# All input products as Strassen quads, with the attention steps between them: a gated hybrid decoder layer on one NeuronCore

## The chip, the cores and the metric

The kernel runs on one core of one Trainium2 chip. A core has TensorE (PE in the profile, its weight loads PEld), VectorE (DVE), ScalarE (ACT), GpSimd (POOL) and SyncE (SP, which here only issues DMAs), an on-chip memory SBUF and the accumulators of TensorE, PSUM, in eight banks of 128 x 512 fp32. The metric is the device time of one execution in microseconds (us); lower is better.

## The reference

One layer is computed, for 2048 tokens of width 1024, in fp32:

```
shift, scale, gate = SiLU(c) @ W_ada + b_ada
u = x * (1 + scale) + shift
[q | k | v | attn_gate | pool_in | pool_gate | merge_a | merge_p] = u @ W_in
A = SlidingWindowGQA_with_sinks(q, k, v; relative bias) * SiLU(attn_gate)          -> @ W_attn_proj
P = (GroupLinear(MultiScaleCausalPool(pool_in)) * pool_scale) * SiLU(pool_gate)    -> @ W_pool_proj
y = (sigmoid(merge_a) * A + sigmoid(merge_p) * P) @ W_out * (1 + gate)
out = LayerNorm(alpha * x + y)
```

Attention has 16 query heads of 64 and 2 key/value heads, a window of 128 tokens and a sink per head. The pool windows are 2, 4, 8 and 16 tokens, one for each quarter of the width.

## The kernel before, in words

**Precision.** TensorE works in fp32r, a rounded fp32. So each operand is split into a rounded part hi and a residue lo, and each product of a 128 x 128 weight tile with 128 x 512 columns takes three matmuls, hi*hi, hi*lo and lo*hi (`mm3`, line 137). ScalarE makes hi by a copy, VectorE makes lo by a subtraction (`low`, line 131).

**Strassen quads.** A `Quad` (line 276) takes two output tiles of 128 columns of a weight and 1024 tokens: a 2 x 2 problem in the halves of the inner width (1024 = 2 x 512) and of the tokens. Strassen's form (Winograd's variant) needs 7 products instead of 8; a product (line 339) is 4 slices of 128 times 3 matmuls, 12 matmuls of 512 columns. The moving side stands in seven sets, B11, T1, T2, B21, T3, B22 and T4, each 128 x 4 x (hi, lo) x 512; the weight side is summed by GpSimd (`sum1`, `mid`, `late`, lines 296 to 306) and split just before use (`pair_split`, line 326, and `half_split`, line 332). `front` opens a quad with the products of B11 and T1, `back` does T2, B21, T3, B22 and T4 and hands the four output tiles to a `consume` function. `ring` (line 447) runs groups of two quads; after each product it calls a tick, and a table of hooks by group and tick places all side work (lines 451 to 458). `defer` puts something off by a number of ticks.

**Stages.** The 2048 tokens are two chunks of 1024. For each chunk:
- a gate stage (`first_phase`, `second_phase`): 17 quads, one for k and v and 16 for the four gates; outputs of the gates pass through a sigmoid (line 545) and go to DRAM. In the first chunk the ticks also carry the folding of the pool-mix weights into the pool-input weights (`fold_parts`, kept split in DRAM as `wmix_d`), the rest of the gate modulation and the split sets of the second chunk (`sums_to` with `kept_parts`). In the second they carry the split sets of the output weight and of the first chunk's attention output (`resplit`).
- an attention stage (`attention`, line 724): 64 steps, one per pair of heads and block of 128 queries, with scores, exponentials, normalisation, transposes and the product with v passing through a pipeline of steps. Into each step goes half of a plain projection (`projection`, line 694: 8 slices of 3 matmuls for one tile of 128 columns and 512 tokens): the q tiles and the folded pool-input tiles, 32 per chunk. For this stage k and v stay in SBUF (`kk`, `vv`), and B11, B21, T2 and B22 hold the plain halves of u. Window sums, gating and the Strassen sums of both outputs run on GpSimd (lines 763 to 814).

Then five mix phases run in one ring each: attention and pool projection of chunk 0, the same of chunk 1 (4 quads each, times the merge gates read back from DRAM), and the output product with the LayerNorm (8 quads). From phase to phase the seven sets are exchanged while the last group still runs (`set_steps`, line 488): raw halves come into two spare rooms and are split from there into the sets; where a store already holds split parts (u of chunk 1, attention of chunk 0, the output weight) a half comes as one load of 1 MB (`fill_set`, line 201).

**Order.** Where operations go through `act`, `dve`, `pool`, `pe` and `sp` they stay in program order among themselves (class `Ordered`, line 50); those through `nc.scalar`, `nc.vector` and so on may be moved by the scheduler. Line 56 is therefore the line of most rows of the profile, and tile names tell them apart: `w_set` is a split weight, `set_T`/`set_B` a moving set, `mm`, `lg`, `pt` and `pv` are PSUM tiles (four, two, one and one banks), `L` holds the logits, `ptl` the residue of the transposed probabilities.

## Time and profile before

| what | value |
|---|---|
| time, three runs | 1781.38 us median (1779.84 to 1782.57) |
| profiled execution, first to last instruction (span) | 1776.8 us; the page gives no time of its own around it |
| TensorE busy, 8248 matmuls | 1711.0 us, 96% |
| VectorE, ScalarE, GpSimd busy | 67%, 52%, 45% |
| DMA | 381.31 MB, 215 GB/s on average |
| granted TensorE clock, mean | 0.989 |

A page of the profile lists the busy time of each engine, the span in 40 slices, the DMA queues, the chain of work that ended last, and groups of equal instructions: line, engine, operation, output<-input by tile names, shapes and count, then busy time and mean duration in ns, then the idle time of the engine just before them and what ended it. Other views list the same for a stretch of time, what an engine waited for, and the instructions in order of time. Matmuls overlap in the pipeline, so a matmul's mean duration is longer than the distance from one to the next.

### The profile page before, as it was taken

What the parts mean: (1) busy time and instruction counts of PE and PEld (TensorE: products, weight loads), DVE (VectorE), ACT (ScalarE), POOL (GpSimd) and SP (SyncE); (2) the same over time, 40 slices, a digit from 0 to 9 for tenths busy, and PEclk for the clock granted to TensorE, in tenths of its full rate; (3) what the DMA queues carried; (4) which work ended last, traced back from release to release, by engine and by line L of the source; (5) the groups of instructions that cost most, each with busy time, mean ns of one, the idle gap of its engine ahead of it and who ended that gap; (6) DMA issues with size and microseconds to landing.
All of it is one profiled execution on the core that took longest, in us unless ns stands there. A gap on an engine that the chain in (4) does not pass through costs nothing. (4 is left out here: it accounts for less than half of the span.)

```text
span 1776.8 us, 24983 instructions
## 1 busy us (share of the span) xinstructions
PE 1711.0 (96%) x8248; PEld 1431.2 (81%) x8248; DVE 1199.1 (67%) x2180; ACT 931.5 (52%) x1969; POOL 795.5 (45%) x610
## 2 busy tenths in 40 slices
PE   6899999999999999999999999999989989999996
PEld 5687888888888887788788888888877868788785
DVE  5866665655777787767655367777857686865777
ACT  3543444445777776454444377777734333423451
POOL 3144454441356567534434025456743552364542
PEclk9899999999999999999999999999999999999998
DMA  9265768743354557787776724554886575689432
GB/s 365 98 238 201 256 218 276 255 174 131 113 166 144 171 202 283 269 289 252 257 276 246 247 79 144 165 166 131 296 307 226 184 253 183 219 312 384 168 143 96
DMA packets 181155, 381.31 MB, mean 215 GB/s; under 512 B 18833, under 2 KB 39329, under 8 KB 181025
## 3 DMA queue, kind: packets, MB, share of 16 engines
q1 hardware_dynamic: 174880, 365.76, 59.1%
q0 software_dynamic: 2912, 9.46, 1.4%
q10 hardware_dynamic: 3232, 4.49, 0.9%
q8 instruction: 65, 1.06, 0.2%
q14 instruction: 66, 0.53, 0.1%
HBM read 244.35 MB, written 138.44 MB: 215 GB/s over the span
## 5 line engine op out<-in xcount | busy, mean ns | idle before, releaser
L56 PE MATMUL mm<-set_B,w_set 128*128 128x512 f32 x3240 | 802.3, 396 | 11.8 <-DVE w_set L132 9.0
L56 PEld LDWEIGHTS mm<-set_B,w_set 128*128 128x128 f32 x3240 | 604.5, 189 | 141.8 <-DVE w_set L132 16.0
L56 PE MATMUL lg<-set_T,w_set 128*128 128x512 f32 x2088 | 511.3, 395 | 22.8 <-DVE w_set L132 12.7
L56 PEld LDWEIGHTS lg<-set_T,w_set 128*128 128x128 f32 x2088 | 392.6, 190 | 115.6 <-DVE w_set L132 18.2
L132 DVE TENSOR_TENSOR w_set<-W,w_set 128x1024 fp32r<-128x1024 f32 x162 | 224.7, 1387 | 177.7 <-ACT w_set L328 169.2
L328 ACT CAST w_set<-W 128x1024 fp32r<-128x1024 f32 x162 | 169.8, 1050 | 242.1 <-PE mm L56 182.5
L56 PE MATMUL mm<-set_T,w_set 128*128 128x512 f32 x1080 | 268.7, 397 | 1.3 <-DVE set_T L56 1.3
L56 PEld LDWEIGHTS mm<-set_T,w_set 128*128 128x128 f32 x1080 | 201.9, 190 | 44.2 <-DVE set_T L56 3.0
L297 POOL TENSOR_TENSOR W<-W,A 128x512 f32<-128x512 f32 x56 | 84.8, 1514 | 247.0 <-DMA A<-in_win_dram 66.6
L306 POOL TENSOR_TENSOR W<-W 128x512 f32<-128x512 f32 x56 | 82.0, 1465 | 160.8 <-DVE w_set L132 146.5
L56 DVE TENSOR_TENSOR o<-pv,o 64x128 f32<-64x128 f32 x256 | 72.4, 283 | 92.1 <-ACT o L56 89.3
L56 ACT ACTIVATE L<-L,nm 128x257 f32<-128x257 f32 (+1 forms) x256 | 127.1, 498 | 9.0 <-DVE nm L56 3.6
L301 POOL TENSOR_TENSOR W<-W 128x512 f32<-128x512 f32 x56 | 88.2, 1576 | 82.8 <-DVE w_set L132 73.7
L56 DVE CUSTOM_DVE_ANT_0 L<-lg,bt,nsink 128x256 f32<-128x256 f32 (+1 forms) x256 | 111.6, 473 | 5.3 <-PE lg L56 1.3
L302 POOL TENSOR_TENSOR W<-W 128x512 f32<-128x512 f32 x56 | 87.3, 1558 | 36.4 <-DMA W<-in_win_dram 26.5
L56 POOL TENSOR_TENSOR w_set<-W,w_set 128x1024 fp32r<-128x1024 f32 x14 | 33.7, 2405 | 139.3 <-ACT w_set L56 96.7
L56 ACT COPY o<-pv 64x256 f32<-64x256 f32 x128 | 47.3, 370 | 82.1 <-PE pv L56 81.5
L56 POOL TENSOR_TENSOR p<-nxt,pg 128x512 f32<-128x512 f32 x32 | 41.5, 1298 | 107.1 <-DVE sm L56 104.2
L56 DVE TENSOR_TENSOR ptl<-pt,pth 128x512 fp32r<-128x512 f32 (+1 forms) x128 | 85.7, 669 | 1.6 <-ACT pth L56 1.4
L56 PE MATMUL lg<-kk,qs 128*128 128x256 f32 (+1 forms) x512 | 80.5, 279 | 0.0
L56 ACT ACTIVATE L<-L,sm 128x256 f32<-128x256 f32 (+1 forms) x128 | 64.3, 502 | 29.5 <-DVE sm L56 29.5
L56 DVE TENSOR_TENSOR k_lo<-spare,k_hi 128x512 fp32r<-128x512 f32 x61 | 61.5, 1014 | 26.1 <-ACT k_hi L56 14.4
(203 smaller groups left out, 2297.1 us busy)
## 6 DMA issues: line engine op xcount, KB each, us to landing
W<-in_win_dram SPq DMA_DIRECT2D x46, 512.0 KB, 5.0
w_set<-wmix_d SPq DMA_DIRECT2D x32, 512.0 KB, 5.2
W<-in_win_dram SPq DMA_DIRECT2D x38, 256.0 KB, 3.4
A<-in_win_dram SPq DMA_DIRECT2D x34, 256.0 KB, 5.0
ag_d<-sig SPq DMA_DIRECT2D x32, 256.0 KB, 3.4
pg_d<-sig SPq DMA_DIRECT2D x32, 256.0 KB, 3.7
ma_d<-sig SPq DMA_DIRECT2D x32, 256.0 KB, 4.1
mp_d<-sig SPq DMA_DIRECT2D x32, 256.0 KB, 3.9
```

The lines of the kernel that those rows point to most:

```text
L56: return lambda *args, **kw: self.tc.keep_in_program_order(op(*args, **kw))
L132: engine.tensor_tensor(dst, src, as32(hi), ALU.subtract)
L297: e.tensor_tensor(self.w[:, 1, :], self.w[:, 2, :], self.a22, ALU.add)
L301: e.tensor_tensor(x[:, 1, :], x[:, 1, :], x[:, 0, :], ALU.subtract)
L302: e.tensor_tensor(x[:, 2, :], x[:, 0, :], x[:, 2, :], ALU.subtract)
L306: e.tensor_tensor(x[:, 3, :], x[:, 3, :], x[:, 1, :], ALU.subtract)
L328: a.copy(by_two(hi), raw)
```

## The change

- **Sets.** The seven sets stay in SBUF from the start. `turn_sets` exchanges them: the raw half is loaded straight into the lo part of its set and split in place some ticks later. All stores are raw; `kept_parts`, `resplit`, `fill_set` and the set B12 go.
- **Quads.** The q tiles and the pool-input tiles become quads (`q_quad`, `mix_quad`); the projections go. 25 quads a chunk: four at the start, 13 alone, eight at the end. `wmix_d` is kept raw.
- **Attention.** The 13 quads alone run one after another in `solos`, with their engines in a written order; after each product a `beat` runs an attention step (`overlay`) when enough credit has gathered, 64 steps over the ticks less ten. q, k, v and the pool input go through DRAM; the keys and values of one key/value head are in SBUF at a time, loaded anew in the middle. The score bank is one instead of two, the product banks five instead of four.
- **Pool.** Window sums and gating move to the eight merge-gate quads at the end of the chunk (`pool_job`), as do the sets of chunk 1; those of the output weight go to the start of chunk 1, all unsplit.
- **Gates.** The sigmoid is computed as (1 + tanh(x/2))/2: gates store tanh or (1 + tanh) * x, the factors 1/2 ride on v, on the pool scale and on the output gate, and the readers add 1 (`scalar_tensor_tensor` in place of `tensor_tensor`).
- **Ring of tiles.** Output tiles come from one ring of three for all stages (five in the mix phases; before, five in each).

```diff
-    sets = {n: set_tile(cp, n) for n in ("B11", "T1", "B21")}
+    sets = {n: set_tile(n) for n in ("B11", "T1", "B21")}
...
-        return ps.tile([P, CH], F32, tag=tag, bufs={"mm": 4, "lg": 2, "pt": 1, "pv": 1}[tag], name=tag)
+        return ps.tile([P, CH], F32, tag=tag, bufs=5 if tag == "mm" else 1, name=tag)
...
+    def solos(ph, quads, nxt, beat):
...
+        w = pair_split(ph, seq[0].first())
+        seq[0].mid()
+        for i, q in enumerate(quads):
+            hi, lo = ph.split(), ph.split()
+            act.copy(by_two(hi), q.second())
+            low(dve, by_two(lo), q.second(), by_two(hi))
...
+            pool_late(pool)
+            ws = halves(hi, lo)[::-1]
+            a, b = bank(), bank()
+            product(a, w[0], "B11", True)
+            c = bank()
+            act.copy(c, a)
+            tick()
+            product(b, w[1], "T1", True)
+            p5 = ph.p("p5")
+            act.copy(p5, b)
+            tick()
+            hi, lo = ph.split(), ph.split()
+            act.copy(by_two(hi), q.third())
+            low(pool, by_two(lo), q.third(), by_two(hi))
+            wt = halves(hi, lo)[::-1]
+            product(c, ws[1], "T2")
+            dve.tensor_tensor(b, c, p5, ALU.add)
+            tick()
+            product(a, ws[0], "B21")
+            q.consume(ph, 0, 0, a)
+            tick()
+            wl = half_split(ph, q.a22, act, dve)
+            product(c, wt[1], "T3")
+            dve.tensor_tensor(p5, c, p5, ALU.add)
+            q.consume(ph, 1, 1, p5)
...
+            tick()
...
+                act.copy(by_two(hi), seq[i + 1].first())
+            product(b, wt[0], "B22")
...
+                low(dve, by_two(lo), seq[i + 1].first(), by_two(hi))
+                seq[i + 1].mid(pool)
...
+            q.consume(ph, 0, 1, b)
+            tick()
+            product(c, wl, "T4")
+            q.consume(ph, 1, 0, c)
+            tick()
+        return [front(ph, q, tick) for q in nxt]
...
+    TURNS = (
+        ("B11", 0, 3), ("T1", 1, 5), ("T2", 3, 7), ("B21", 4, 9), ("T3", 7, 11), ("B22", 8, 13), ("T4", 10, 16),
     )
...
+        def raw(name, half):
+            sp.dma_start(as32(sets[name][:, 2 * half : 2 * half + 2, 1, :]), store[name][half])
+
+        def split(name, half):
+            t = sets[name][:, 2 * half : 2 * half + 2]
+            act.copy(t[:, :, 0, :], as32(t[:, :, 1, :]))
+            low(dve, t[:, :, 1, :], as32(t[:, :, 1, :]), t[:, :, 0, :])
...
+    def q_quad(s, m):
+        def consume(ph, mi, t, src):
+            hi, lo = ph.c("q_hi", F32R), ph.c("q_lo", F32R)
+            on["act"].activation(hi, src, AF.Copy, scale=-0.125)
+            on["dve"].scalar_tensor_tensor(lo, src, -0.125, as32(hi), ALU.mult, ALU.subtract)
+            defer(2, lambda: [sp.dma_start(q_d[s, m + mi, t, n], as32(x)) for n, x in enumerate((hi, lo))])
...
-            nc.scalar.activation(g, src, AF.Sigmoid)
...
+            on["act"].activation(g, src, AF.Tanh, scale=0.5)
+            if full:
+                on["dve"].scalar_tensor_tensor(g, g, 1.0, src, ALU.add, ALU.mult)
...
+        def step(n):
+            if n - 3 in xs:
+                values(n - 3)
+            lg = scores(n) if n < N else None
+            pt = transposes(n - 2) if 0 <= n - 2 < N else None
...
+        def beat():
+            n, credit, rest = at
+            at[1] += N / (n_ticks - 10.0)
+            if rest:
+                at[2] -= 1
+            elif at[1] >= 1 and n < N + 3:
+                step(n)
+                at[0] += 1
+                at[1] -= 1
+                if n == N // 2 - 1:
+                    load_k(1)
+                    at[2] = 2
+                if n == N // 2 + 2:
+                    load_v(1)
+                    at[2] = 1
...
+        start = [[kv_quad(s), q[0]], [ag[0], pg[0]]]
+        alone = [q[2], ag[2], q[4], ag[4], q[6], ag[6], pg[2], x[0], x[2], x[4], x[6], pg[4], pg[6]]
+        end = [[ma[0], ma[2]], [ma[4], ma[6]], [mp[0], mp[2]], [mp[4], mp[6]]]
...
+        for j in range(KT):
+            at(0, 7 + j // 4, lambda j=j: spread_bias(j))
+        for g in range(4):
+            steps(hooks, groups, (3, 7, 11, 15)[g], fold_parts(ph, g))
+        for i in range(8):
+            steps(hooks, groups, 6 + 2 * i, gate_modulation(ph, 2 * KT + i, cb))
```

More of the change, by code (lines that the diff above doesn't have):

```diff
@@ new lines @@
+    attn0 = pairs(lambda m: attn_quad(0, m))
+    opened = None
+    for s in range(2):
+        start, alone, end = chunks[s]
+        if s == 0:
+            with Pools("g0", spare=2, x=3) as ph:
+                first_chunk_start(ph, start, alone)
+        else:
+            with Pools("g1", spare=9) as ph:
+                second_chunk_start(ph, opened, start, alone)
+        with Pools(f"o{s}") as ph:
+            pin(True)
+            beat, finish_up = overlay(ph, s, 7 * len(alone) + 4)
+            opened = solos(ph, alone, end[0], beat)
+            finish_up()
+            pin(False)
+        with Pools(f"e{s}", spare=4, pg=2, st=5) as ph:
+            nxt, store = (attn0[0], ain_d[0]) if s else (chunks[1][0][0], u1_d)
+            opened = chunk_end(ph, s, opened, end, nxt, store)
@@ L1409 @@
+    with Pools("mix", spare=1, more=2) as ph:
         phases = []
```

976 lines of the change are left out of this document (406 added, 570 removed).

## The prediction

> **What bounds the kernel now.** I read the page first (busy time, then the costliest groups), then the chain of waits, then TensorE's own timeline inside an attention stage, then a table of busy times by stage, and last what TensorE waited for.
>
> ```profile
> span 1776.8 us, 24983 instructions
> ...
> PE 1711.0 (96%) x8248; PEld 1431.2 (81%) x8248; DVE 1199.1 (67%) x2180; ACT 931.5 (52%) x1969; POOL 795.5 (45%) x610
> ...
> L56 PE MATMUL mm<-set_B,w_set 128*128 128x512 f32 x3240 | 802.3, 396 | 11.8 <-DVE w_set L132 9.0
> ...
> L56 PE MATMUL lg<-set_T,w_set 128*128 128x512 f32 x2088 | 511.3, 395 | 22.8 <-DVE w_set L132 12.7
> ...
> L56 PE MATMUL mm<-set_T,w_set 128*128 128x512 f32 x1080 | 268.7, 397 | 1.3 <-DVE set_T L56 1.3
> ```
>
> TensorE is busy 96% of the span: 65.8 us of idle in all. The three groups are the products with 512 columns, 3240 + 2088 + 1080 = 6408 of them. That count can be checked against the code: a Strassen quad is 7 products of 4 slices of 3 matmuls, 84; 34 quads for the gates and k, v and 24 in the mix phases make 4872; the q and pool-input projections (lines 694 to 704) are 2 chunks x 16 tiles x 48 = 1536.
>
> The pace of such a matmul where nothing holds it up is read from the chain of waits (start, duration, what), which merges the 12 matmuls of one product:
>
> ```profile
> 1466.96 2.72 PE lg L56 x12
> 1469.68 2.72 PE mm L56 x12
> ```
>
> Each product starts 2.72 us after the one before: 226.7 ns a matmul. The attention step's share comes from TensorE's timeline in an attention stage (start, duration):
>
> ```profile
> 575.69 3.00 PE L56 MATMUL mm<-set_B,w_set 128*128 128x512 f32 x12
> ...
> 579.84 3.02 PE L56 MATMUL mm<-set_T,w_set 128*128 128x512 f32 x12
> ```
>
> From product to product 4.15 us, of which 2.72 is the product: a step of attention (scores, transposes, values) costs TensorE 1.43 us. Next the stages:
>
> ```profile
> 44.00:133.00 89.00, 78.73 (x358) 63.27 (x358) 68.20 (x93) 45.85 (x72) 24.28 (x20) 0.90 0.48 168
> 489.00:666.00 177.00, 176.89 (x1013) 154.48 (x1012) 137.83 (x421) 133.81 (x405) 104.19 (x86) 1.00 0.52 171
> 689.00:755.00 66.00, 61.70 (x270) 49.85 (x269) 47.07 (x58) 32.50 (x53) 35.96 (x25) 0.97 0.74 271
> ...
> 1286.00:1333.00 47.00, 42.02 (x188) 33.35 (x188) 25.84 (x39) 15.96 (x27) 22.97 (x18) 1.00 0.84 312
> 1422.00:1466.00 44.00, 37.71 (x154) 29.19 (x154) 35.20 (x32) 17.23 (x20) 26.59 (x16) 0.96 0.80 256
> ```
>
> The columns are stretch, length, then TensorE, weight load, VectorE, ScalarE and GpSimd busy, clock, DMA share, GB/s. In the attention stage (second row) TensorE never idles, with VectorE at 137.83/177 = 78% and ScalarE at 76%. So only TensorE work, or a wait of TensorE, moves the time. The waits sit in the head, in the tail, and where the seven sets are exchanged: 66 - 61.70 = 4.3, 5.0 and 6.3 us in the last three rows.
>
> **The change part by part.**
>
> (a) *q and pool input as quads.* Per chunk, 16 tiles of 48 matmuls become 8 quads of 84: 768 - 672 = 96 fewer, 192 in both chunks. 192 x 226.7 ns = **-43.5 us**. Attention keeps 64 steps per chunk with the same matmuls, the folding of the pool weights keeps its matmuls too, and 24 mix quads stay as they are.
>
> (b) *The exchange of the sets.* Before, each half was loaded into one of two spare rooms and split from there, or came split in a load of twice the size. Afterwards the raw half lands in the set itself as soon as its last reader is through, three to six ticks (2.72 us each) ahead of the split.
>
> ```profile
> set_T<-u_T_split SPq DMA_DIRECT2D x8, 1024.0 KB, 7.6
> spare<-ain_T SPq DMA_DIRECT2D x16, 512.0 KB, 4.6
> ```
>
> A lead of three ticks, 8.2 us, covers 4.6 us to landing; the old lead of about one tick did not. What TensorE waited for says which part can go (wait; us, times, longest):
>
> ```profile
> PE lg L56 <- DVE w_set L132: 12.7, 9, 5.8
> ...
> PE lg L56 <- DMA set_T<-ain_T_split: 3.0, 2, 2.8
> PE lg L56 <- DMA set_T<-u_T_split: 2.6, 2, 2.1
> ```
>
> At most the 15.6 us of the three exchange rows go; at least nothing, since six exchanges now need splits on ScalarE and VectorE where three did. I take **-10**, near the upper end because the DMA behind the wait has its lead.
>
> (c) *Attention between single quads.* This is the dear part. Thirteen quads per chunk run alone, 7 products each, with 64 steps over 95 - 10 = 85 ticks: 0.753 a tick, 5.27 a quad. TensorE: 7 x 2.72 + 5.27 x 1.43 = 26.6 us a quad. To see whether VectorE and ScalarE keep up, I take a step's cost from the attention stage by leaving out what is not attention (x | busy, mean ns):
>
> ```profile
> L56 DVE TENSOR_SCALAR L<-L,sm 128x256 f32<-128x256 f32 x37 | 26.7, 722 | 0.0
> ...
> L56 DVE SCALAR_TENSOR_TENSOR qs<-mm,qs 64x512 fp32r<-64x512 f32 x22 | 15.2, 689 | 8.9 <-ACT qs L56 8.8
> ...
> L56 ACT ACTIVATE qs<-mm 64x512 fp32r<-64x512 f32 x22 | 12.9, 585 | 0.1
> ...
> L56 ACT COPY L<-nsink 128x2 f32<-128x2 f32 x43 | 8.5, 197 | 0.0
> ...
> L56 DVE SCALAR_TENSOR_TENSOR nxt<-nxt,mm 128x512 f32<-128x512 f32 x11 | 7.5, 679 | 1.5 <-POOL nxt L56 1.5
> ...
> L56 ACT COPY vb<-mm 128x512 f32<-128x512 f32 x11 | 6.2, 565 | 0.0
> L56 ACT CAST w_set<-W 128x1024 fp32r<-128x1024 f32 x6 | 6.2, 1031 | 0.0
> ```
>
> 43 steps lie in that stretch (the sink copy, one a step). VectorE: (137.83 - 15.2 - 7.5) / 43 = 2.68 us a step. ScalarE: (133.81 - 12.9 - 8.5 - 6.2 - 6.2) / 43 = 2.33 (the sink copy moves to GpSimd). The quad's own operations, over the whole run:
>
> ```profile
> L132 DVE TENSOR_TENSOR w_set<-W,w_set 128x1024 fp32r<-128x1024 f32 x162 | 224.7, 1387 | 177.7 <-ACT w_set L328 169.2 <-issue 4.1 <-PE mm L56 1.9
> L328 ACT CAST w_set<-W 128x1024 fp32r<-128x1024 f32 x162 | 169.8, 1050 | 242.1 <-PE mm L56 182.5 <-POOL W L297 28.9 <-POOL wide L574 9.8
> ...
> L132 DVE TENSOR_TENSOR w_set<-A,w_set 128x512 fp32r<-128x512 f32 x58 | 53.4, 941 | 17.4 <-ACT w_set L335 15.7 <-PE lg L56 1.6
> ...
> L386 DVE TENSOR_TENSOR mm<-lg,p 128x512 f32<-128x512 f32 x58 | 40.2, 694 | 9.8 <-PE lg L56 8.0 <-ACT p L384 1.3
> ...
> L545 ACT ACTIVATE sig<-mm 128x512 f32<-128x512 f32 x64 | 37.9, 592 | 12.4 <-DMA wmix_d<-st_hi 6.9 <-PE mm L56 3.5 <-DMA ma_d<-sig 1.2
> ...
> L56 POOL TENSOR_TENSOR w_set<-W,w_set 128x1024 fp32r<-128x1024 f32 x14 | 33.7, 2405 | 139.3 <-ACT w_set L56 96.7 <-PE lg L56 42.6
> ...
> L549 DVE SCALAR_TENSOR_TENSOR sig<-mm,psc,sig 128x512 f32<-128x512 f32 x16 | 11.9, 742 | 2.0 <-ACT sig L545 2.0
> ```
>
> VectorE per q or gate quad: two residues of 1.39 (the third is GpSimd's, 2.41), one of 0.94, two sums of 0.69 and four outputs of 0.74: 8.1 us, plus 5.27 x 2.68 = 14.1: 22.2 of 26.6, 83%. ScalarE: three casts of 1.05, then seven operations of 0.59: 7.3 + 12.3 = 19.6, 74%. Neither is the bound by its sum, but VectorE stands 5 points above the 78% that left TensorE without a gap, both run in a fixed order, and the score, transpose and value banks are now one each (the score bank was two).
>
> What queues behind a wait: after a T3 product VectorE waits for it, does the sum (0.69), waits for ScalarE's output copy (0.59), writes the residue (0.74), and only then normalises, scores and residues of the step behind it (2.68): about 4.9 us after T3's end with the hand-overs. The next step may not reuse the transpose bank before that, and TensorE comes to it 1.43 + 2.72 = 4.15 us after T3's end, plus about 1.1 for values and scores. So one such step just fits. With three steps running at the T3, B22 and T4 ticks, ScalarE's next cast (1.05) and VectorE's next residue (1.39) come between as well and the lag grows past the bank by a little over 1 us. Ticks without a step (one in four) let it recover. I take 0.5 us a quad, **+13** over 26 quads; the lower bound is nothing (the attention stage above has none), the upper 3 us a quad, +78, as if such a lag came at each of the three ticks.
>
> (d) *The second half of k and v.* After step 31 the keys of the other head group are loaded over the first, two ticks without a step; 1 MB landed in 7.6 us in the row above, two ticks are 5.4. About 2 us each chunk: **+4**, bounds 0 and 12.
>
> (e) *Edges of the lone stage.* The first quad after it is split only behind its last product: 1.05 + 1.39 = 2.4 us twice, and the same where it begins, if nothing is moved ahead of it. Half of the 9.8: **+5**, bounds 0 and 10.
>
> (f) *The squeezed start.* Chunk 0 now folds the pool weights, multiplies the gate modulation and finishes the head's sets beside 4 quads instead of 17.
>
> ```profile
> L56 DVE CUSTOM_DVE_ANT_0 spare<-spare,cb,mod 128x1024 f32<-128x1024 f32 x4 | 8.0, 2010 | 0.0
> ...
> L56 DVE TENSOR_TENSOR room_k<-spare,room_k 128x1024 fp32r<-128x1024 f32 x4 | 4.9, 1226 | 2.9 <-ACT room_k L56 2.9
> ```
>
> VectorE: 8 x 2.0 for the modulation, 8 x 1.23 + 4 x 0.74 for the folding, about 9 for twelve half-width operations of the head (0.74 each), 4 x 9.5 for the quads (three residues here): 76 us, against 4 x 19.04 = 76 us of products and the folding's own matmuls. The old row 44:133 had VectorE at 77% and lost 10 us. Besides, q, k and v leave as two tiles each through a ring of three, so a copy can wait for a store. I take +8 for chunk 0 and +3 for chunk 1, **+11**; bounds 0 and 40 (that VectorE's work is served with half of it uncovered).
>
> The rest I cost at nothing: the tanh has the sigmoid's shape and the factor rides on operations that stay; the pool's window sums stand beside 152 us of merge-gate products per chunk; saved split copies and stores pay for q, k, v and the pool input in DRAM. If that cover failed, it would show as (c) or (f).
>
> Sum: -43.5 - 10 + 13 + 4 + 5 + 11 = -20.5; 1776.8 - 20.5 = 1756.3 us of span. The page gives no time for its execution around the span; the runs' median, 1781.38, lies 4.6 above the span, and I add that: **1761 us**.
>
> Two rules of the Trainium skill bear on (c). The interleaving rests on tanh and exp needing no table exchange between them; the old run shows what one costs:
>
> ```profile
> L56 ACT ACT_TABLE_LOAD x2 | 2.6, 1283 | 0.0
> ```
>
> The Trainium skill, "ScalarE: Activation LUTs", section "Table sets: the hidden batching unit", puts exp and tanh into one set and the sigmoid into another; no run here shows tanh yet, so the opposite stays a rival, with a small chance. Against the change speaks "SBUF — State Buffer", section "Who interferes with whom": a VectorE operation with two SBUF inputs and a GpSimd operation that reads SBUF shut each other out for a whole instruction. The trace agrees in kind: the scaling of L took 722 ns in the attention stage above (GpSimd 59% busy), and over the whole run
>
> ```profile
> L56 DVE TENSOR_SCALAR L<-L,sm 128x256 f32<-128x256 f32 x120 | 71.6, 597 | 0.0
> ```
>
> The inflated prices are those in my sum; were the exclusion worse with residues on both engines, that would be the first rival.
>
> **The rivals.**
>
> *1. The lag binds (slower).* Place: the lone quads. Price: 2.6 us a quad instead of 0.5, from the in-order chain of (c). It decides from (20.5 + 13) / 26 = 1.3 us a quad; there the gain is gone. At 2.6: 1761 + 26 x 2.1 = 1816. For it: VectorE at 83%, one score bank, a reader on another engine behind every product. Against it: no wait at 78%, and the idle ticks.
>
> *2. Nothing lags.* (c) to (f) cost 4 together and all 15.6 of the exchanges go: 1776.8 - 43.5 - 15.6 + 4 + 4.6 = 1726. For it: the attention stage without a gap, the short landing times. Against: four new places to wait.
>
> *3. The start binds.* (f) at 40 instead of 11: 1790. For it: 76 us of VectorE work beside 76 us of products. Against: the modulation and most of the folding have no reader on TensorE near them.
>
> *4. Tables are exchanged at every gate.* The change would then not do what it says. 12 gate quads x 8 loads x 1.283 us = 123 us on ScalarE, which has 7.0 us free a quad and needs 10.3: from 12 x 3.3 = 40 to 123 us more, 1801 to 1884.
>
> **How the numbers follow.** Forecast 0.42 (1740 to 1776), rival 1 0.24, rival 2 0.20, rival 3 0.11, rival 4 0.03. 0.2% is 3.6 us, about what a measurement of this kernel can tell from no change. Faster by more than that: 0.40 of the forecast, rival 2, 0.01 of rival 1: 0.61. Within: 0.02 of the forecast, 0.02 each of rivals 1 and 3: 0.06. Slower: 0.33. The range runs from 1722 (just under rival 2) to 1822 (just over rival 1); below it is left about 0.06, above it 0.13.
>
> **What would show it.** (a): 6216 matmuls of 512 columns. (b): no DMA among what TensorE waits for at the exchanges. (c): in the lone stage 26.6 to 27.1 us per quad; rival 1 shows over 28 there, with TensorE's waits named by ptl, o or nm of VectorE. (d): a gap of about 2 us at the middle of attention, released by a load of kk. (f): TensorE's idle time from 44 to 160 us; rival 3 shows over 30 us of it. Rival 4 shows some hundred table loads. My number is wrong if the products after a set's exchange still wait, or if the lone quads wait at more than one tick each.

## The result, and the profile after

| | before | after |
|---|---|---|
| time, median of 4 runs each on the same chip | 1781.97 us (1779.84 to 1785.4) | 1880.9 us (1874.38 to 1881.54) |
| ratio of the means | | 1.0545, 95% interval 1.0523 to 1.0567 |
| span of the profiled execution | 1776.8 us | 1878.9 us |
| mean granted TensorE clock | 0.989 | 0.965 |

The change made the kernel 5.5% slower, where 1% faster was forecast. First the page of the changed kernel: span, busy times, and the three groups of products with 512 columns.

```profile
span 1878.9 us, 24883 instructions
...
PE 1721.1 (92%) x8056; PEld 1416.6 (75%) x8056; DVE 1335.6 (71%) x2197; ACT 922.0 (49%) x1756; POOL 882.5 (47%) x738
...
L56 PE MATMUL mm<-set_B,w_set 128*128 128x512 f32 x2664 | 676.5, 403 | 19.6 <-DVE w_set L135 17.3
L56 PE MATMUL mm<-set_T,w_set 128*128 128x512 f32 x2688 | 672.8, 400 | 12.3 <-DVE w_set L135 7.3
...
L56 PE MATMUL lg<-set_T,w_set 128*128 128x512 f32 x864 | 218.4, 400 | 18.2 <-DVE w_set L135 11.7
```

2664 + 2688 + 864 = 6216: the 192 matmuls are gone, and with them 43.5 us. All the same the span is 102.1 us longer, so TensorE must lose 146 us more. What it waited for (us, times, longest):

```profile
PE pv L56 <- DVE st L56: 31.9, 26, 4.4
PE mm L56 <- DVE w_set L135: 24.5, 12, 4.2
PE pv L56 <- ACT room_k L56: 20.2, 3, 16.7
PE lg L56 <- DVE w_set L135: 11.7, 11, 2.7
...
PE pv L56 <- DVE ptl L56: 9.7, 35, 0.3
PE pt L56 <- ACT vt L539: 8.4, 1, 8.4
```

These rows are too small by themselves: behind a wait the granted clock is often half for a while (from 302.9 to 306.3 us behind the wait of 1.96 us shown below), and small hand-overs do not count as waits. So I also sum, over all matmuls from 65 us on, the time from one start to the next less the pace of that kind (226.7 ns with 512 columns, 119.5 with 256, 85.3 with 128), cut at the first and last attention matmul of each chunk and at the first transpose of chunk 1's values; a gap counts in the stage in which it ends. Call it the loss. It was 78.7 us before and is 224.7 after: +146.0, and 146.0 - 43.5 = 102.5, against the 102.1 by which the span grew. By stage, with four later kernels beside it:

| stage (us in the changed kernel) | after | e1 | e5 | e7 | e15 |
|---|---|---|---|---|---|
| start of chunk 0 (66 to 190) | 37.5 | 35.3 | 24.4 | 25.8 | 37.5 |
| lone quads with attention, chunk 0 (190 to 552) | 49.5 | 28.8 | 35.0 | 34.0 | 25.8 |
| end of chunk 0 (552 to 776) | 38.7 | 35.1 | 41.4 | 17.3 | 23.3 |
| start of chunk 1 (776 to 850) | 11.9 | 11.6 | 9.8 | 8.1 | 13.0 |
| lone quads with attention, chunk 1 (850 to 1214) | 52.0 | 29.8 | 35.9 | 39.9 | 26.6 |
| the rest | 35.1 | 33.1 | 33.2 | 34.8 | 35.3 |
| sum | 224.7 | 173.7 | 179.6 | 160.0 | 161.6 |

The old kernel is compared by the same stretches of time, though its work lay otherwise in them: 187 to 560 and 845 to 1215 us lost 9.8 us each and held gate quads first, attention only from 425 and 1024 us on. Its two attention stages as a whole (425 to 693, 1024 to 1295) lost 11.9 and 11.1. 65 to 187 lost 17.5. The new stages in the table of busy times (columns as in the prediction):

```profile
190.00:552.00 362.00, 338.31 (x1768) 283.76 (x1768) 259.49 (x670) 236.44 (x570) 145.83 (x153) 0.98 0.45 143
552.00:776.00 224.00, 200.76 (x821) 158.81 (x820) 168.44 (x138) 78.48 (x111) 157.14 (x114) 0.95 0.76 257
845.00:1214.00 369.00, 344.38 (x1799) 289.61 (x1798) 263.04 (x669) 240.34 (x570) 146.30 (x153) 0.97 0.46 144
```

In the lone stages (rows 1 and 3) VectorE is busy 72% and 71%, yet TensorE waits for it. In the end stage (row 2) VectorE and GpSimd are both over 70%. One step of attention in the lone stage shows how VectorE's order holds TensorE; first VectorE in order of time (start, duration), then TensorE's next instruction:

```profile
296.92 2.09 DVE L56 TENSOR_TENSOR w_set<-W,w_set 128x1024 fp32r<-128x1024 f32 x1 [1.27 <-POOL st L56]
298.93 0.67 DVE L56 SCALAR_TENSOR_TENSOR sig<-sig,mm 128x512 f32<-128x512 f32 x1
299.53 0.15 DVE L56 RECIPROCAL sm<-sm 128x2 f32<-128x2 f32 x1
299.72 0.59 DVE L56 TENSOR_SCALAR L<-L,sm 128x256 f32<-128x256 f32 x1
300.23 0.47 DVE L56 CUSTOM_DVE_ANT_0 L<-lg,bt,nsink 128x256 f32<-128x256 f32 x1
...
301.03 0.57 DVE L56 TENSOR_TENSOR st<-pv,o 64x128 f32<-64x128 f32 x2
301.64 0.69 DVE L56 TENSOR_TENSOR ptl<-pt,pth 128x512 fp32r<-128x512 f32 x1
```

```profile
301.75 0.36 PE L56 MATMUL pv<-pth,vv 128*128 128x256 f32 x1 [1.96 <-DVE st L56]
```

The scaling (TENSOR_SCALAR) and the score reductions stand ahead of the value sums (st<-pv). TensorE's next values need the bank that those sums read, so TensorE stands still for 1.96 us. The kernel before had another order in its step: value sums, scores, the transposes' residue, scaling last.

### The profile page after: what moved, and what is told of

It is laid out like the page before. It is cut to its first block, busy times and chain, and to the rows that moved or that the text cites. A ratio compares the mean times of both kernels' runs of the same rounds, so it can differ in the third digit from the quotient of the medians.

```text
span 1878.9 us, 24883 instructions
## 1 busy us (share of the span) xinstructions
PE 1721.1 (92%) x8056; PEld 1416.6 (75%) x8056; DVE 1335.6 (71%) x2197; ACT 922.0 (49%) x1756; POOL 882.5 (47%) x738
## 4 chain that ended last, share of the span: by engine, by line
PE 39%; DVE 11%; issue 5%; DMA 4%; POOL 3%; ACT 3%; SPq 1%; POOLq 0%; DVEq 0%; ACTq 0%
PE mm L56 30%; PE lg L56 7%; DVE w_set L135 2%; DVE L L56 1%; DVE st L56 1%; POOL nxt L56 1%; PE pv L56 1%; DVE set_T L56 1%; PE pt L56 1%; ACT L L56 1%; DVE nxt L56 1%; DVE w_set L56 1%; POOL st L56 1%; DMA qs<-q_d 1%; ACT w_set L56 1%
## 5 line engine op out<-in xcount | busy, mean ns | idle before, releaser
L56 PE MATMUL mm<-set_B,w_set 128*128 128x512 f32 x2664 | 676.5, 403 | 19.6 <-DVE w_set L135 17.3
L56 PE MATMUL mm<-set_T,w_set 128*128 128x512 f32 x2688 | 672.8, 400 | 12.3 <-DVE w_set L135 7.3
L56 PEld LDWEIGHTS mm<-set_B,w_set 128*128 128x128 f32 x2664 | 509.3, 194 | 133.7 <-DVE w_set L135 21.1
L56 PEld LDWEIGHTS mm<-set_T,w_set 128*128 128x128 f32 x2688 | 506.6, 191 | 124.1 <-DVE w_set L135 8.9
L135 DVE TENSOR_TENSOR w_set<-W,w_set 128x1024 fp32r<-128x1024 f32 x142 | 210.4, 1483 | 111.3 <-ACT w_set L290 96.0
L56 PE MATMUL lg<-set_T,w_set 128*128 128x512 f32 x864 | 218.4, 400 | 18.2 <-DVE w_set L135 11.7
L56 PEld LDWEIGHTS lg<-set_T,w_set 128*128 128x128 f32 x864 | 163.7, 191 | 60.7 <-DVE w_set L135 16.5
L262 POOL TENSOR_TENSOR W<-W,A 128x512 f32<-128x512 f32 x46 | 72.5, 1576 | 180.8 <-ACT vt L539 49.5
L56 DVE TENSOR_TENSOR w_set<-W,w_set 128x1024 fp32r<-128x1024 f32 x54 | 70.6, 1308 | 55.6 <-ACT w_set L56 38.4
L56 DVE TENSOR_SCALAR L<-L,sm 128x256 f32<-128x256 f32 (+1 forms) x128 | 103.8, 811 | 4.6
L56 PE MATMUL pv<-pth,vv 128*128 128x256 f32 x248 | 69.1, 294 | 34.2 <-DVE st L56 31.9
L56 DVE TENSOR_TENSOR set_T<-set_T 128x1024 fp32r<-128x1024 f32 x48 | 83.2, 1734 | 7.9 <-ACT set_T L56 7.8
L56 POOL TENSOR_TENSOR st<-st,ag 128x512 f32<-128x512 f32 x32 | 41.4, 1295 | 100.3 <-DVE st L56 72.3
```

The lines of the kernel that those rows point to most:

```text
L56: return lambda *args, **kw: self.tc.keep_in_program_order(op(*args, **kw))
L135: engine.tensor_tensor(dst, src, as32(hi), ALU.subtract)
L262: e.tensor_tensor(self.w[:, 1, :], self.w[:, 2, :], self.a22, ALU.add)
```

## The experiments

Each later kernel ran beside the old one on its own chip; there the old one's median lay between 1782.0 and 1783.9 us, so differences of 2 to 4 us between later kernels are not read. Three theories at first. A: VectorE's order within a step. B: the ring of three output tiles and the stores that are put off by two ticks. C: the single bank of the values.

**e1, e2: the order put back; each store put off by one tick instead of two** (`defer(0)` acts at the next tick). The order of e1 in words:

```
-  reciprocal; act: scale E0; dve: scale E1; ...; scores; value sums; residue
+  reciprocal; value sums; act: scale E0; ...; scores; residue; dve: scale E1     (e1)
-            defer(2, lambda: [sp.dma_start(q_d[...]) ...   and four alike
+            defer(0, lambda: [sp.dma_start(q_d[...]) ...                          (e2)
```

> The attention step's operations of VectorE go back to the order of the kernel before: the value sums (which free the value bank) and the residue of the transposed probabilities ahead, the scaling of the second head's exponentials last. Theory A (the order binds: in the lone stages TensorE reaches the next step's values before VectorE has got through scaling and scores to the value sums): most of the 37.8 us of TensorE waits named 'DVE st' and of the 18 us of half-clock behind them in the two lone stages go; 1881 - 40 = about 1840 us. Theory B (the ring of three output tiles binds: VectorE stands before it ever gets to the step, for a store to land): these waits shrink by a third at most, 1865 to 1880 us. Theory C (one bank of each kind binds): the waits for 'DVE st' go over to 'DVE ptl' and the time stays within 5 us of 1881.

> The stores of q, k, v, gates and pool input are issued one tick after their tile is made instead of two, so that they stand ahead of more of SyncE's other work. Theory B (the ring of three output tiles binds): VectorE's waits for q_d, k_d and v_d stores shrink, the 17 us hole at 87 to 104 us in the first stage and the 8.5 us hole at 787 to 796 us shrink to half or less, and the long waits of the lone stages (4.4 us at 277) go: 1881 - 30 = about 1850 us. Theory A (the order of the step binds): only the holes of the two first stages go, 1865 us. If SyncE's in-order waiting is the greater evil (an earlier store now blocks the loads behind it), the time stays or grows.

Measured: e1 1829.49 us, ratio to before 1.0266 (1.0246 to 1.0286), 51 us less than the change, where theory A forecast 40; e2 1870.28, 1.0491 (1.0464 to 1.0518), 11 us less. In e1 the two lone stages together lose 43 us less (table), and TensorE's waits for the value sums are gone. A holds. The scaling itself grew cheaper in its other place; VectorE's rows of chunk 0's lone stage, the change first, then e1:

```profile
L56 DVE TENSOR_SCALAR L<-L,sm 128x256 f32<-128x256 f32 x56 | 47.0, 839 | 2.0
```

```profile
L56 DVE TENSOR_SCALAR L<-L,sm 128x256 f32<-128x256 f32 x56 | 29.0, 518 | 0.0
```

Its price hangs on GpSimd. Over the whole run, the scalings of this size that run beside no tensor_tensor of GpSimd take 0.36 us on average in the changed kernel and 0.35 in e1. Those that run beside one take 1.14 (72 of 120) and 0.82 (51 of 120).

In e2 the start of chunk 0 loses 28.8 instead of 37.5, the lone stages nothing less (107.3 against 101.5): B is an affair of the start, and the time is nearer to A's 1865 than to B's 1850.

**e3: two banks for the values, four instead of five for the products.** This version no longer computes the layer; its instructions are the same in kind, and it is read for the waits alone.

```
-    bufs=5 if tag == "mm" else 1
+    bufs={"mm": 4, "lg": 1, "pt": 1, "pv": 2}[tag]
...
-    c = bank("mm" if x else "lg")      (and once more in the ring)
+    c = bank("pv" if x else "lg")
```

> Two banks for the values and four for the products (the second quad of a pair takes its third accumulator from the value banks). Theory C (one bank binds): the waits of values for 'DVE st' (31.9 us) go, 1881 - 35 = about 1845 us. Theory A and B: the values then wait for the residue 'ptl', which VectorE makes after the value sums of the same step, so at most the 0.6 us between the two is gained at each of some 30 places, about 1865 us.

Measured: 1875.6 us, 1.0521 (1.0493 to 1.0548), 5 less. C falls, and its waits view says why: the wait for the value sums goes, the next instruction in VectorE's order takes its place (9.7 us in the changed kernel). The 1865 of A and B is not reached either; what the product bank given up costs is not parted from it.

```profile
PE pv L56 <- DVE ptl L56: 33.1, 41, 1.6
```

**e4: other partners in the first two groups.**

```
-        start = [[kv_quad(s), q[0]], [ag[0], pg[0]]]
+        start = [[kv_quad(s), ag[0]], [q[0], pg[0]]]
```

> In each chunk's first two groups q's first quad changes places with the first attention-gate quad, so that only k and v, not q as well, draw two tiles per output from the ring of three in the first group. Theory B: the holes at 87 to 104 us and 787 to 796 us shrink, 10 to 25 us less than 1881. Theory that the first stage is bound by VectorE's work (rival 3 of the prediction): the same work in the same stage, within 5 us of 1881.

Measured: 1887.93 us, 1.0592 (1.0566 to 1.0618), 7 more: a miss. The start of chunk 0 loses 50.8 instead of 37.5, that of chunk 1 4.8 instead of 11.9. Why the first grew was not traced.

**e9, e10: the halves of the order.**

```
 e9:  only the scaling of E1 moved to the end of the step
 e10: only the value sums (and ScalarE's copy for them) moved ahead of the scores
```

> The changed kernel with one instruction a step moved: VectorE's scaling of the second head's probabilities goes from right behind the reciprocal to the end of the step, where the kernel before had it. It takes 871 ns a piece in the changed kernel and 509 in the run with the whole order put back, 128 of them: 46 us of VectorE. Theory A1 (the scaling is the part of the order that counts, by its place ahead of the scores and by its price): 30 us or more of the 51 come back, 1851 or less, and the scaling's mean falls below 600 ns. Theory A2 (the value sums behind the scores are the part that counts, since VectorE waits for the score matmuls ahead of them): less than 15 us come back, 1866 or more.

> The other half of the order: the value sums (and ScalarE's copy for them) ahead of the score reductions, the scaling left behind the reciprocal and so still ahead of the scores. Theory A2: 30 us or more of the 51 come back, 1851 or less, and TensorE's waits for the value sums (31.9 us) go. Theory A1: TensorE then waits for the transposes' residue instead, as it did with a second value bank, and less than 15 us come back, 1866 or more. The two halves together must give about 51.

Measured: e9 1843.1 us, 1.0347 (1.0307 to 1.0387), 38 less; e10 1865.88, 1.0472 (1.0439 to 1.0505), 15 less; together 53, against the whole order's 51. A1 holds in the time: the dear part is one scaling ahead of the scores. Its second sign just misses: the scaling falls to 609 ns in e9's lone stage of chunk 0, not below 600. In e10, as in e3, TensorE waits for the residue instead:

```profile
PE pv L56 <- DVE ptl L56: 31.4, 47, 1.8
```

**e5, e6: order and stores together; then the bias copies spread.** The later ones are variants of e5 or e1.

```
 e5: e1 and e2
 e6: e5, and
-            at(0, 7 + j // 4, lambda j=j: spread_bias(j))
+            at(1, j, lambda j=j: spread_bias(j))
```

> Both earlier edits together: VectorE's step order of the kernel before (value sums first, scaling last), and each output tile stored at the tick in which it is made. They gave -51 and -11 us alone. If they act at different places they add: 1881 - 51 - 11 = 1819 (1812 to 1826). If both were the same cure (a shorter way to the attention's values in the lone stage) nothing is added: 1829. This run is also the base of the next three, which each differ from it in one thing. In it the start of chunk 0 (65 to 187 us) should still lose 30 to 35 us of TensorE against the pace of its products, the end of chunk 0 (560 to 780 us) about 40, the two lone stages 20 to 30 each.

> The base with the eight 384 KB copies of the bias, which ScalarE's queue issues at ticks 7 and 8 of the first group, issued one a tick through the second group. Theory D: the hole of 17 us near 87 us is DMA traffic: the DMA share is 0.95 there against 0.56 just before, a 256 KB store takes about 8 us instead of 2.5, and everything of the three-tile ring queues behind it. Then the hole shrinks to under 6 us, and the time falls by 10 to 18 us against the base. Theory R: the hole is the order of the ring and of SyncE's queue (k, v, q share three tiles), whatever the traffic. Then the time stays within 4 us of the base and the hole stays over 12 us.

Measured: e5 1839.97 us, 1.031 (1.0269 to 1.0351), outside both expected numbers: 10 us more than e1. e6 1836.16, 1.0289 (1.025 to 1.0327). By the table, e5 against e1: the start gains 11 us, the lone stages lose 12 again and the end of chunk 0 loses 6. In the lone stage SyncE, whose issues keep the program's order, waits longer at stores whose tiles aren't ready (for ScalarE's px and q tiles 84.6 us from 190 to 530, 58.0 in e1), and loads behind them come late; TensorE's waits in e5 (in e1 the queries cost it 6.0 us, and the values are not among its waits):

```profile
PE pv L56 <- DMA vv<-v_d: 10.4, 3, 5.6
...
PE lg L56 <- DMA qs<-q_d: 9.0, 2, 6.9
```

The hole of the start, 85 to 105 us, where TensorE stands still longest, in the changed kernel, in e5 and in e6:

```profile
85.00:105.00 20.00, 3.02 (x12) 2.00 (x10) 5.69 (x7) 5.78 (x8) 3.78 (x3) 0.66 0.95 303
```

```profile
85.00:105.00 20.00, 12.35 (x56) 10.40 (x55) 5.66 (x7) 5.63 (x8) 3.85 (x3) 0.74 1.02 331
```

```profile
85.00:105.00 20.00, 16.00 (x78) 13.52 (x77) 9.50 (x11) 7.89 (x11) 5.34 (x5) 0.91 0.92 287
```

TensorE is busy for 3.0, 12.4 and 16.0 us of the 20, at a DMA share of 0.95, 1.02 and 0.92. In the changed kernel ScalarE and VectorE wait there for stores to land, whose tiles the ring of three needs again; the four of q and v that are issued from 81 to 91 us, 256 KB each, land after 7.8 to 8.5 us, where the medians of q's stores are 2.9 and 2.3:

```profile
98.74 0.63 ACT L547 ACTIVATE q_hi<-p 128x512 fp32r<-128x512 f32 x1 [5.68 <-DMA v_d<-v_lo]
```

```profile
97.59 0.69 DVE L135 TENSOR_TENSOR k_lo<-mm,k_hi 128x512 fp32r<-128x512 f32 x1 [4.21 <-DMA v_d<-v_hi]
```

So late stores and the bias traffic both make the hole (its one long wait is 16.7, 7.2 and 3.2 us). But the start as a whole loses 24.4 us in e5 and 24.2 in e6, so what closes the hole is lost again elsewhere in the stage. Theory D is right on the hole and misses its 10 to 18 us of time; theory R, which kept the hole, is right on the time alone.

**e7, e8, e11: the end of chunk 0.** All three are e5 with one thing changed.

```
 e7:  window sums of chunk 0 left out (GpSimd's 40 adds and 4 products), the value read in their place
 e8:  modulate(): dve.tensor_scalar(u, ...) -> act.activation(u, u, AF.Identity, ...)
 e11: window sums of chunk 0 computed as ever, but the value read in their place
```

> The base with the pool's window sums of chunk 0 left out, so that part of the output isn't the reference's: the pool branch of chunk 0 uses the value itself in place of its window sum. GpSimd loses some 36 adds (about 50 us) in the end stage of chunk 0, VectorE keeps all its instructions. Theory P: VectorE and GpSimd shut each other out at SBUF for whole instructions. Then VectorE's residue of a weight pair in 610 to 750 us falls from 1.57 us to under 1.40 with no change of its own, the loss of TensorE in 560 to 780 falls from about 42 us to under 20, and the run is 20 to 30 us faster than the base. Theory Q: VectorE's own queue is too long there and GpSimd only adds the waits for its sums (12.5 us of VectorE's idle). Then the residue keeps 1.5 us or more and the gain is 8 to 13 us. If neither, the gain is under 5.

> The base with the modulation of chunk 1's input (eight instructions of 128x1024, 1.41 us each on VectorE in the end stage of chunk 0) moved to ScalarE, which is busy 36% of that stage. VectorE loses 11 us of 126. Theory P (shut out by GpSimd): each of VectorE's instructions there is prolonged by what GpSimd holds, so 11 us of its own work are worth about as much in TensorE's waits: -8 to -14 us. Theory Q (VectorE's queue): the same 11 us, -8 to -11. If the waits of TensorE in that stage are set by GpSimd alone (sums of weights ready too late), the gain is under 4 us. ScalarE's own casts may come later by up to 1.2 us at eight places: +0 to +5.

> The kernel with the order put back and stores at once (1840.0 us), in which GpSimd still computes all window sums of chunk 0, but VectorE reads the value itself in their place, so that part of the output isn't the reference's. VectorE and GpSimd keep all their instructions; only VectorE's wait for GpSimd's sums goes (20.6 us of its idle time in 600 to 745 us). Without the sums on GpSimd the kernel was 26 us faster. Theory P (GpSimd's work itself slows VectorE and the weight sums): most of that stays away, the gain is under 8 us. Theory W (VectorE, in order, waits for the window sums while the weight residues stand behind): the gain is 15 to 26 us, and VectorE's residue of a weight pair still takes 1.5 to 1.6 us.

Measured: e7 1814.05 us, 1.0162 (1.0127 to 1.0197), 26 less than e5; e8 1834.07, 1.0272 (1.023 to 1.0314), 6 less, short of the 8 that both theories asked and hardly outside what e5 varies; e11 1832.12, 1.0274 (1.0248 to 1.0299), 8 less, P by a hair. In the table the end of chunk 0 falls from 41.4 to 17.3 in e7. So the sums cost some 25 us, of which VectorE's wait for them is at most 8; the rest comes with GpSimd's work itself. VectorE's groups from 600 to 745 us in e5, then in e11:

```profile
L135 DVE TENSOR_TENSOR w_set<-W,w_set 128x1024 fp32r<-128x1024 f32 x17 | 26.9, 1589 | 8.3 <-ACT w_set L290 8.3
L56 DVE SCALAR_TENSOR_TENSOR nxt<-nxt,vb 128x512 f32<-128x512 f32 x11 | 14.8, 1343 | 20.6 <-POOL nxt L56 10.7 <-POOL vb L56 9.9
```

```profile
L135 DVE TENSOR_TENSOR w_set<-W,w_set 128x1024 fp32r<-128x1024 f32 x19 | 33.0, 1743 | 6.0 <-ACT w_set L290 6.0
...
L56 DVE SCALAR_TENSOR_TENSOR st<-vb 128x512 f32<-128x512 f32 x11 | 15.2, 1380 | 0.0
```

20.6 us of waiting are gone, and the residues behind them take 1743 ns instead of 1589. Over the whole end of chunk 0 VectorE's busy time grows from 167.8 to 181.5 us with the same instructions, so most of the time spared in the wait comes back as longer instructions. P has a second way as well: GpSimd's weight sums come later. ScalarE's casts wait for them 20.5 us in that stage of e5, 32.8 in e11 and 12.4 in e7. These runs do not part the two ways. One part of P missed: in e7 the residue fell to 1454 ns, not under 1400; GpSimd's weight sums stay there.

**e12: what seemed to help, together.** e1 with e6's and e8's edits and the window sums started one tick earlier.

> What helped, together, with the whole computation kept: the order put back (1829.5 us), the bias copies spread over the second group (-4), the modulation on ScalarE (-6), and the window sums of each pool job started one tick earlier so that VectorE waits less for them (theory W: -8 to -12; theory P: 0 to -3). Stores stay deferred, since at once they cost 10 us in this order. Theory W 1809 (1803 to 1815), theory P 1818 (1814 to 1825). None of it touches the rest of the start, so the kernel before (1782) should stay ahead by over 1%.

Measured: 1835.89 us, 1.029 (1.0256 to 1.0324): 6 more than e1 (4 by the ratios), a miss for both theories. The end of chunk 0 loses 40.3 us (35.1 in e1). Together, work started earlier and work moved to ScalarE brought nothing there.

**e13, e14: the two disputed costs by themselves.**

```
 e13: VectorE's residue, scaling and difference from a bank, 24 each, alone; GpSimd's
      24 adds alone; then each of the three beside 24, 16 and 16 adds
 e14: e1, beat() returns at once; the attention steps run behind the lone quads
```

> None of the reference's computation: 24 of VectorE's residues (128x1024, two inputs in SBUF), 24 scalings (128x256, one input in SBUF) and 24 differences with one input from a bank (128x512) alone, then 24 of GpSimd's adds (128x512, SBUF) alone, then each of VectorE's kinds beside GpSimd's adds, all on tiles of their own that nothing waits for. Theory P: the two engines shut each other out at SBUF. Then the residue beside the adds rises from about 1.2 us to the sum of both, over 1.8, and the add from about 1.05 to as much, while the difference with an input from a bank (0.69) rises less. Theory Q: the longer means in the kernel's end stage come from something else there (DMA traffic, a wait inside the instruction). Then all means beside the adds stay within 10% of those alone.

> The kernel with the order put back, and the attention of a chunk run behind its 13 lone quads instead of between their products; the same instructions. Its time is no measure, since attention alone leaves TensorE idle (64 steps a chunk). What counts is the lone quads by themselves, 13 x 7 products at 2.72 us = 247.5 us a chunk. Theory I: the remaining loss of the lone stages (30 and 22 us with the order put back) is the meeting of quads and attention on VectorE and ScalarE. Then the quads alone lose under 8 us a chunk. Theory S: it is the quads' own chain (casts, residues and sums for one quad at a time, one bank for each sum). Then they lose 15 us or more a chunk without any attention.

e13 in order of time (start, duration of the row's 24 or 16 instructions), one execution; VectorE first, GpSimd below. The first three rows and the first GpSimd row are alone, the others beside each other:

```profile
5.07 30.21 DVE L56 TENSOR_TENSOR lo<-W,hi 128x1024 fp32r<-128x1024 f32 x24 [3.57 <-ACT hi L56]
...
35.77 9.30 DVE L56 TENSOR_SCALAR L<-V,sm 128x256 f32<-128x256 f32 x24
...
45.56 17.37 DVE L56 TENSOR_TENSOR Y<-acc,V 128x512 f32<-128x512 f32 x24
...
95.64 52.80 DVE L56 TENSOR_TENSOR lo<-W,hi 128x1024 fp32r<-128x1024 f32 x24
...
148.86 24.47 DVE L56 TENSOR_SCALAR L<-V,sm 128x256 f32<-128x256 f32 x24
...
173.75 17.36 DVE L56 TENSOR_TENSOR Y<-acc,V 128x512 f32<-128x512 f32 x24
```

```profile
63.33 32.08 POOL L56 TENSOR_TENSOR g<-g,g 128x512 f32<-128x512 f32 x24
...
95.49 51.87 POOL L56 TENSOR_TENSOR g<-g,g 128x512 f32<-128x512 f32 x24
...
148.71 21.37 POOL L56 TENSOR_TENSOR g<-g,g 128x512 f32<-128x512 f32 x16
...
173.60 21.44 POOL L56 TENSOR_TENSOR g<-g,g 128x512 f32<-128x512 f32 x16
```

Per instruction: the residue 30.21/24 = 1.26 us alone, 2.20 beside the adds, and the add 1.34 alone, 2.16 beside the residue. The pair takes 2.2 us where one after the other would take 2.60. The scaling takes 0.39 alone. Its second row mixes two prices: the 16 scalings beside adds start 1.34 us apart, one for each add, and the last 8 run alone again at 0.39; the adds keep their 1.34. The difference with an input from a bank stays at 0.72, and the adds beside it at 1.34. P holds. The Trainium skill, "SBUF — State Buffer", section "Who interferes with whom", says the same of which kinds meet: two inputs in SBUF, or a scaling in a mode that uses both of VectorE's SBUF ports, against GpSimd's reads, but not one input beside a bank. All three pairs agree on the kinds. Shutting out for whole instructions, as the prediction has the rule, would give the first pair 2.60, and 2.2 was measured.

e14, the 13 lone quads of chunk 0 without attention between them:

```profile
180.00:441.00 261.00, 261.00 (x1141) 213.77 (x1139) 85.28 (x104) 95.65 (x136) 103.47 (x72) 1.00 0.40 130
```

TensorE has no gap at all; the loss from 182 to 441 us is 2.8 us, against 28.8 in e1 with the same quads and attention between. Theory I holds: the quads by themselves lose next to nothing, the loss comes where attention meets them. (Attention by itself leaves TensorE idle, with no products between its steps, so that half is no measure.)

**e15, e16, e17: work moved from GpSimd to the busier VectorE,** each on e1.

```
 e15: chunk 0's window sums and the differences of chunk 1's input: pool -> dve
 e16: low(pool, by_two(lo), q.third(), by_two(hi)) -> low(dve, ...)
 e17: both
```

> The kernel with the order put back (1829.5 us), with chunk 0's window sums (40 adds and four small products) and the differences of chunk 1's input (16) moved from GpSimd to VectorE; all is computed. VectorE, the busier of the two there (80% against 74% in 560 to 760 us), gets 56 more instructions of about 0.68 us, 38 us; GpSimd loses 56 of 1.34 us alone, 75 us. Theory P (SBUF serves one of the two at a time): what counts is the sum of both, which falls by 37 us, so the end of chunk 0 loses 15 to 30 us less: 1800 to 1815, and VectorE's residues there fall from 1.57 us towards 1.25. Theory Q (VectorE's own queue is the bound): 38 us more on it make the stage slower by 10 to 30 us: 1840 to 1860.

> The kernel with the order put back, and the lone quads' third residue (26 of 128x1024) moved from GpSimd to VectorE. GpSimd loses 26 of about 2.4 us, VectorE gets 26 of about 1.25 us, in a place of its fixed order ahead of the quad's first sum. Theory P: the scalings beside it shrink from 0.51 us towards the 0.39 that they take alone, the lone stages lose 5 to 15 us less each: 1800 to 1820. Theory Q (VectorE's order and load): +1.25 us a quad in the order that already holds the transposes' bank, 26 x 0.5 to 26 x 1.25: 1842 to 1862.

> Both moves together. They act in different stages, so they add: theory P 1771 to 1805, at its lower end a kernel ahead of the one before (1782), theory Q 1850 to 1890.

Measured: e15 1817.62 us, 1.019 (1.0175 to 1.0206), 12 less than e1; e16 1837.73, 1.0304 (1.028 to 1.0327), 8 more; e17 1826.62, 1.0231 (1.0205 to 1.0257), outside both expected ranges. In the end of chunk 0 Q is out and P has the direction, with 12 us and not the 15 to 30 expected: the loss falls from 35.1 to 23.3 although VectorE got 60 more instructions, and its residue (600 to 745 us) falls from 1590 ns to

```profile
L135 DVE TENSOR_TENSOR w_set<-W,w_set 128x1024 fp32r<-128x1024 f32 x19 | 24.6, 1293 | 2.7 <-ACT w_set L291 2.7
```

ScalarE's wait for GpSimd's weight sums is the same there (17.7 us, 17.5 in e1), so the gain hardly comes from them. But VectorE's wait for GpSimd's sums, 14.6 us in e1, is gone too, so e15 does not single out the shorter instructions. In the lone stages (e16) neither theory held. The loss stays where it was (27.1 and 32.0; 28.8 and 29.8 in e1): GpSimd's third residue is not what binds there. The 8 us were not traced to a stage; the two profiled executions differ by 4.3. e15 is the fastest with the whole computation, and still 1.9% slower than before: it may lose 78.7 + 43.5 = 122 us to draw level and loses 161.6. No version ahead of the old kernel was found.

## Why the prediction was wrong

It gave 1761 us with a range up to 1822; the time is 1880.9. The loss by its own terms, each against the same stretch of time in the old kernel:

- **(a)** was right: 6216 matmuls, -43.5 us at the pace of 226.7 ns.
- **(b)** -10 for the exchanges of the sets: not seen. No load is among TensorE's waits there, as forecast, but the rest, with the end of chunk 1, loses 35.1 us where 1215 us to the end lost 28.0 before.
- **(c) is the step that failed.** 0.5 us a quad and +13 were taken; the two lone stages lose 101.5 us where the same stretches lost 19.6, so 82 us more, or 3.1 a quad, just past the upper bound of 3. A lone quad takes 28.9 and 29.4 us from first product to next in the two chunks, over the 28 that rival 1 named as its sign; the waits that it named are there too, for the value sums 31.9 us and for ptl 9.7. Rival 1 was the right mechanism at too small a price. The working had it that "one such step just fits" from one old duration of each instruction, and read from VectorE's 83% that it would keep up. It took a step's instructions as one sum behind the quad's, not each in its own place. Their order within the step was new, and by e1, e9 and e10 it holds 43 of the 82 us in these stages (51 in the run), most of it through one scaling ahead of the scores. The scaling was priced at 722 ns; it took 839 in the lone stage of chunk 0, 518 with the order put back. The prediction took 722 against 597 as a trace of the rule on two inputs in SBUF, but a scaling reads one; what a scaling pays beside GpSimd, e13 shows. The other 39 us come from the meeting of quads and attention (e14). Which instruction's place holds them stays open: in e1's first lone stage TensorE's named waits add up to 9.6 of the 28.8 us.
- **(d)** 4 us: the second keys are not among TensorE's waits; one wait of 4.2 us for a load of queries is. **(e)** 5 us was not separated from (c).
- **(f)** +11 with bounds 0 to 40: 37.5 against 17.5 in 65 to 187 us, and 11.9 in the start of chunk 1, where the old kernel lost 0.5, so up to 32 us. That is rival 3's place and nearly its price, but its reason was another. VectorE was busy 64 us of the 122 from 65 to 187 and stood waiting for stores in the hole: its sum did not bind. Stores through the ring of three, at a DMA share of 0.95, did in part, which (f) named without a price of their own: stores a tick earlier give back 9 to 11 of the 20 us in chunk 0 (e2, e5). The rest of that stage stays open.
- **"The rest at nothing"** failed at the pool's window sums. TensorE had products to cover them, but VectorE and GpSimd had no time to spare: the end of chunk 0 loses 38.7 us, 13.1 in that stretch before, and some 25 hang on those sums (e7). The Trainium skill's rule ("SBUF — State Buffer", section "Who interferes with whom") was weighed in (c), where moving a residue gained nothing (e16), and not here, where both engines are over 70% busy.
- **Rival 4** is out: the run has one table load in all. That its 1801 to 1884 us hold the measured time is chance.

```profile
L944 ACT ACT_TABLE_LOAD x1 | 1.3, 1283 | 0.7 <-PEq L1395 0.7
```

Together: 82 for the lone stages, 32 for the two starts, 25 for the end of chunk 0 and 7 for the rest make 146 us more loss, as measured.

## What to carry to other kernels

When steps of one pipeline are laid between products of another, write out the order of the in-order engine instruction by instruction, and put what frees a bank ahead of what nobody waits for; the engine's busy share says nothing of it. Where VectorE and GpSimd both work from SBUF, add their times and compare the sum with the stage. A sum past the stage is a warning and no more: it was 326 us in the 224 of the end stage, but also 242 in the 177 of the old attention stage (489 to 666), where TensorE lost nothing. Work moved to the busier but faster of the two can then make the stage shorter (e15).

## What the hardware showed beyond that

A scaling of 128x256 takes 0.39 us alone and 1.34 beside GpSimd's adds, one for each add, with no loss to the adds. The residue and the add that meet both slow down (1.26 to 2.20 and 1.34 to 2.16). And a wait is paid more than once: in the changed kernel the clock is granted at half in 24 spells, all but the last a multiple of 3.4 us long (7 spells before), most of them at a wait or within a few us of it. Of the 225 us lost some 39 are the extra time of matmuls that start in such spells, 8 of 79 before.
